# Seven products in place of eight for some blocks of a two-layer encoder's projections

## The chip, the core and the metric

The kernel runs on one core of one Trainium2 chip, and the metric is its device time in microseconds. A core has engines that work side by side, each through its own list of instructions in order: TensorE (PE) multiplies a stationary block of 128 x 128 with a moving one of up to 512 columns and adds into a bank of PSUM; VectorE (DVE) and ScalarE (ACT) work element by element; GpSimd (POOL) fills, masks and issues transfers here; SyncE (SP) issues transfers. Transfers are carried by 16 DMA engines. Engines wait for one another by semaphores. In shapes, 128x512 means 128 partitions with 512 elements each.

## What is computed

A trunk of one layer A and one layer B on x of 256 x 2048, all in float32, with 32 heads of 128 and an inner width of 4096:

```
h = rms_norm(x, a_norm);  q, k, v, g = split(h @ a_w_in, 4)          # 2048 -> 4 x 4096
o = chunked_relbias_attention(q, k, v, rel_bias)                     # chunks of 64, band of 9 chunks
x = x + (o * silu(g)) @ a_w_out                                      # 4096 -> 2048
h_kv = rms_norm(x, kv_norm);  k, v = split(h_kv @ kv_w, 2)
logf = log_sigmoid(h_kv @ f_w + f_b);  cum = cumsum(logf)
q, g = split(rms_norm(x, b_norm) @ b_w_in, 2)
o = forgetting_attention(q, k, v, cum)                               # causal, blocks of 128 queries
x = x + (o * silu(g)) @ b_w_out
return rms_norm(x, final_norm)
```

## The kernel before

**Matmuls.** Every float32 operand of a projection is split into a high part (rounded, type fp32r) and a low part (the rest), and a product is three matmuls: high by high, high by low, low by high. `mm3` (line 174) does this for one slice of 128 of the contraction and both halves t of the 256 rows; line 182 is the matmul, with the activations stationary and 512 columns of weights moving.

**Units and sub-blocks.** A *unit* (`Unit`, line 300) is one output of 256 x 512 in two PSUM banks. Its weights come in *sub-blocks* b of two slices (KB = 2), 512 KB each, so a sub-block is 2 slices x 2 halves x 3 = 12 matmuls. Layer A has 16 *pairs* of units g: `aqk` (q and k of two heads) and `avg` (v and gate of the same heads), eight sub-blocks each; layer B has 16 pairs `bqg` and `bkv`. The output projections of A (`ao`) and B (`bo`) are four units of sixteen sub-blocks. A matmul whose tile is called `aqk_acc` belongs to an aqk unit.

**Weights.** `Feed` (line 186) runs a fixed list of all sub-blocks. `begin` lets SP load one into one of RAW = 3 load buffers (line 203). `prepare` splits it into one of SPLIT = 4 pairs of split buffers: ACT copies the high part (line 237), DVE subtracts the low part (line 238); in layer B a gain is multiplied in (lines 232 and 233). `get` keeps four prepared ahead, so a split is written three sub-blocks before its matmuls and waits until PE has left the buffer.

**Attention beside the projections.** `attention` (line 394) is a generator; each `yield` ends a step, and tables (lines 55 to 61) say after which sub-block of a later unit how many steps are written. For a pair of layer A: qk is copied out of the banks by ACT with the row scale (`evac_scaled`, line 367); `turn` (line 355) transposes blocks of 32 on DVE (line 360) and sends 16 transfers (line 363), here 12 by POOL and 4 by ACT; q and k are split (lines 382, 383); PE does the scores s1p and s0p (lines 390 to 392, 414); DVE adds the bias and takes the maximum (421, 422); ACT does exp (424); the sums are inverted and the gate scaled (430 to 435); probabilities and gate are turned with 16 transfers of POOL (tiles sgY, sgZ); the probabilities are split; PE does the product with v (op, lines 390 to 392 and 448); DVE and ACT write the result (452 to 457). `close_vg` (line 559) splits v and forms the gate when the avg unit is complete. Scores stand behind the last avg sub-block (`QK_STEPS`), the second turn is written behind sub-block 1 of the next aqk unit (`PV_STEPS`), the split and op behind sub-blocks 0 and 2 of the next avg unit (`OLD_A_STEPS`). `feed.behind` (line 252) ties a split of attention to the weights' split before it.

**Order.** The source gives the order in which instructions are written. The builder (the Tile framework) then orders each engine's list, places tiles in their slots and sets the semaphores.

**Projections.** `project` (line 332) runs a list of sub-blocks with other generators beside it. `ao_closed` (line 623) adds x, stores x1 and turns it into the operand of layer B; the last unit is transposed on PE at once (`x_to_T`, lines 160 and 167). For the last bo unit the second half of its last eight sub-blocks is held back, so that the first half's rows are finished under it.

Of the kernel before, what the change touches and what calls it, by code (L numbers as in the profile page):

```python
# [16 lines left out]
P = 128  # L17
S = 256
# [23 lines left out]
RAW = 3  # L42
# [8 lines left out]
TERMS = 8  # L51
HEAT = 9
WAIT = 8

QK_STEPS = {0: 1, 6: 1, 7: 2}
PV_STEPS = {1: 1}
# [17 lines left out]
def trunk(ctx, tc, x, x_t, gains, a_w_in, a_rel, a_w_out, kv_w, f_w, f_b, b_w_in, b_w_out, final_norm, out):  # L74
# [99 lines left out]
    def mm3(acc, lhs, k, ts, hi, lo, nk, begun):  # L174
# [5 lines left out]
        for t, i in steps:  # L180
            x, w = parts[i]
            pe.matmul(acc[t], x[:, t * P:(t + 1) * P], w,  # L182
                      start=t not in begun, stop=k == nk - 1 and i == 2)
            begun.add(t)

    class Feed:
# [8 lines left out]
        def load(self, spec, b, first):  # L195
            if self.early:
                raw = self.early.pop(0)
            else:
                raw = stream.tile([P, IL, KB, HN], F32, name=f"{spec['name']}_raw{b}", tag="raw", bufs=RAW)
# [6 lines left out]
        def begin(self, first=None):  # L206
            spec, b = next(self.todo, (None, 0))
            if spec:
# [5 lines left out]
        def prepare(self, ahead=True, parts=(slice(None),)):  # L214
# [30 lines left out]
        def refill(self):  # L245
            while len(self.loaded) < RAW:
# [20 lines left out]
    def spec(name, w, nk, late=0, kept=0, g0=None):  # L267


        return dict(name=name, w=w, nk=nk, late=late, kept=kept, g0=g0)  # L270

    def whole(spec):
        return [(spec, b) for b in range(spec["nk"] // KB)]

    qkvg = []
    for g in range(NG):
        qkvg.append(spec(f"aqk{g}", a_w_in[2 * g], KD))
        qkvg.append(spec(f"avg{g}", a_w_in[2 * g + 1], KD))
# [3 lines left out]
    for sp_ in qkvg[2:]:  # L282
        todo += whole(sp_)
    ao = [spec(f"ao{u}", a_w_out[u], KI) for u in range(4)]
    for sp_ in ao:
        todo += whole(sp_)
# [6 lines left out]
    ao_order = [i for sp_ in ao for i in whole(sp_)]  # L293
    bo_order = [i for sp_ in bo for i in whole(sp_)]
    bo_order.insert(KI // KB + WAIT, bo_order.pop(KI // KB - 1))
    todo += bo_order
# [3 lines left out]
    class Unit:  # L300
# [3 lines left out]
        def __init__(self, lhs, sp_):  # L304
            self.lhs, self.nk, self.late = lhs, sp_["nk"], sp_["late"]
            self.acc = [ps_acc.tile([P, UN], F32, name=f"{sp_['name']}_acc{t}", tag="acc") for t in range(NT)]
            self.held, self.left, self.begun = [], self.nk // KB, set()

        def step(self, b):
            hi, lo = feed.get()  # L310
            hold = b >= self.nk // KB - self.late
            if hold:
                self.held.append((b, hi, lo))
            for j in range(KB):
                mm3(self.acc, self.lhs, b * KB + j, range(1 if hold else NT), cols(hi, j), cols(lo, j), self.nk,
                    self.begun)
# [532 lines left out]
```

## Time and profile before

| | us |
|---|---|
| median of three runs | 1760.83 |
| the three runs | 1760.07, 1760.83, 1763.58 |
| the profiled execution, device time | 1762.27 |
| its span in the trace | 1760.4 |

The granted clock of PE in the profiled execution is 0.998 of full speed. The program moves 396.34 MB, a mean of 225 GB/s. The page gives busy time of each engine, a chain of work followed back from the last instruction, and groups of instructions; the trace can be asked for who waited for whom, for instructions in order of time, and for the busy time of each engine in a stretch. A row such as `L369 ACT ACTIVATE qk<-bkv_acc,rstd_b 128x256 f32<-128x256 f32 x32 | 15.0, 473 | 11.4 <-PE` is: 32 instructions of line 369 on ACT, 15.0 us busy, 473 ns each, and 11.4 us in which the engine had stood idle just before them, ended by PE. PE's busy time counts overlapping matmuls, so the spacing of their starts is the better measure.

### The profile page before, as it was taken

How to read it: one execution, taken by the hardware profiler on the slowest of the kernel's cores; microseconds unless marked ns; L12 is line 12 of the kernel's file. 1: busy time of each engine (PE TensorE's matmuls, PEld its weight loads, DVE VectorE, ACT ScalarE, POOL GpSimd, SP SyncE). 2: the span in 40 equal slices, each digit the busy share in tenths (PEclk: the TensorE clock that was granted, in tenths of full speed). 3: DMA queues.
4: the chain of work that ended last, by engine and by line, in shares of the span. 5: the costliest groups of instructions: out<-in, count | busy, mean ns of one | idle time of the engine just before them, and what ended most of it. 6: DMA issues, size and time to landing. Idle time of an engine off the chain costs nothing.

```text
span 1760.4 us, 25526 instructions
## 1 busy us (share of the span) xinstructions
PE 1746.0 (99%) x8387; PEld 1533.1 (87%) x8387; DVE 1159.1 (66%) x1662; ACT 1084.1 (62%) x2063; POOL 515.7 (29%) x1071
## 2 busy tenths in 40 slices
PE   9999999999999999999999999999999999999997
PEld 7888888888888888888888888888888888888886
DVE  6666666666666666655666777777777777776654
ACT  6555555555555555555556777777777777765443
POOL 1333333333333333111104333333333333333000
PEclk9999999999999999999999999999999999999999
DMA  7867776777777777777766777777777777776665
GB/s 255 248 218 227 225 225 224 225 224 224 223 224 224 224 225 222 222 239 240 239 195 226 236 227 222 227 224 226 223 228 226 227 222 231 249 225 222 216 217 161
DMA packets 143652, 396.34 MB, mean 225 GB/s; under 512 B 31104, under 2 KB 38560, under 8 KB 143392
## 3 DMA queue, kind: packets, MB, share of 16 engines
q1 hardware_dynamic: 107472, 354.25, 63.8%
q0 software_dynamic: 32256, 37.29, 6.6%
q10 hardware_dynamic: 3792, 3.17, 0.6%
q8 instruction: 66, 1.08, 0.2%
q14 instruction: 66, 0.54, 0.1%
HBM read 351.05 MB, written 4.23 MB: 202 GB/s over the span
## 4 chain that ended last, share of the span: by engine, by line
PE 94%; DMA 2%; DVE 2%; ACT 1%; issue 0%; POOL 0%; SPq 0%; ACTq 0%; DVEq 0%; POOLq 0%
PE bkv_acc L182 19%; PE bqg_acc L182 19%; PE avg_acc L182 18%; PE aqk_acc L182 17%; PE ao_acc L182 9%; PE bo_acc L182 8%; DMA bo_raw<-in_b_w_out 1%; PE op L448 1%; PE s0p L414 1%; PE op L391 0%; PE s1p L390 0%; PE s1p L391 0%; PE op L392 0%; PE op L390 0%; PE s1p L392 0%
## 5 line engine op out<-in xcount | busy, mean ns | idle before, releaser
L363 POOL DMA_DIRECT2D sgZ<-sgY x512 | 250.9, 497 | 194.6 <-DVE sgY L360 96.5
L363 POOL DMA_DIRECT2D turned<-turned x448 | 219.9, 498 | 267.7 <-PE avg_acc L182 93.0
L233 DVE SCALAR_TENSOR_TENSOR bqg_lo<-bqg_raw,gain,bqg_hi 128x512 fp32r<-128x512 f32 x256 | 182.0, 747 | 97.1 <-ACT bqg_hi L232 97.0
L232 ACT ACTIVATE bqg_hi<-bqg_raw,gain 128x512 fp32r<-128x512 f32 x256 | 170.9, 714 | 114.1 <-PE bqg_acc L182 50.2
L238 DVE TENSOR_TENSOR avg_lo<-avg_raw,avg_hi 128x1024 fp32r<-128x1024 f32 x127 | 153.4, 1219 | 115.6 <-ACT avg_hi L237 115.5
L238 DVE TENSOR_TENSOR aqk_lo<-aqk_raw,aqk_hi 128x1024 fp32r<-128x1024 f32 x125 | 152.4, 1219 | 92.7 <-ACT aqk_hi L237 92.6
L233 DVE SCALAR_TENSOR_TENSOR bkv_lo<-bkv_raw,gain,bkv_hi 128x512 fp32r<-128x512 f32 x256 | 181.3, 748 | 45.3 <-ACT bkv_hi L232 42.3
L237 ACT ACTIVATE avg_hi<-avg_raw 128x1024 fp32r<-128x1024 f32 x127 | 132.5, 1055 | 124.5 <-PE aqk_acc L182 60.1
L182 PE MATMUL bqg_acc<-bqg_hi,x1Th 128*128 128x512 f32 x512 | 191.6, 384 | 0.0
L182 PE MATMUL aqk_acc<-aqk_hi,xTh 128*128 128x512 f32 x512 | 190.9, 383 | 0.2
L182 PE MATMUL aqk_acc<-aqk_lo,xTh 128*128 128x512 f32 x512 | 189.0, 379 | 1.2 <-DVE aqk_lo L238 1.2
L182 PE MATMUL avg_acc<-avg_hi,xTh 128*128 128x512 f32 x512 | 190.2, 382 | 0.0
L182 PE MATMUL avg_acc<-avg_lo,xTh 128*128 128x512 f32 x512 | 188.9, 379 | 0.3 <-DVE avg_lo L238 0.3
L182 PE MATMUL bqg_acc<-bqg_hi,x1Tl 128*128 128x512 f32 x512 | 189.1, 379 | 0.0
L182 PE MATMUL bkv_acc<-bkv_hi,x1Th 128*128 128x512 f32 x512 | 189.0, 379 | 0.0
L182 PE MATMUL aqk_acc<-aqk_hi,xTl 128*128 128x512 f32 x512 | 188.9, 379 | 0.0
L182 PE MATMUL avg_acc<-avg_hi,xTl 128*128 128x512 f32 x512 | 188.8, 379 | 0.0
L182 PE MATMUL bkv_acc<-bkv_lo,x1Th 128*128 128x512 f32 x512 | 188.8, 379 | 0.0
L182 PE MATMUL bkv_acc<-bkv_hi,x1Tl 128*128 128x512 f32 x512 | 188.8, 379 | 0.0
L182 PE MATMUL bqg_acc<-bqg_lo,x1Th 128*128 128x512 f32 x512 | 188.8, 379 | 0.0
L237 ACT ACTIVATE aqk_hi<-aqk_raw 128x1024 fp32r<-128x1024 f32 x125 | 131.5, 1052 | 91.9 <-PE avg_acc L182 44.0
L232 ACT ACTIVATE bkv_hi<-bkv_raw,gain 128x512 fp32r<-128x512 f32 x256 | 168.8, 711 | 27.9 <-PE bqg_acc L182 21.4
(205 smaller groups left out, 3442.4 us busy)
## 6 DMA issues: line engine op xcount, KB each, us to landing
bqg_raw<-in_b_w_in SPq DMA_DIRECT2D x128, 512.0 KB, 4.3
bkv_raw<-in_kv_w SPq DMA_DIRECT2D x128, 512.0 KB, 4.0
avg_raw<-in_a_w_in SPq DMA_DIRECT2D x127, 512.0 KB, 4.3
aqk_raw<-in_a_w_in SPq DMA_DIRECT2D x125, 512.0 KB, 3.4
ao_raw<-in_a_w_out SPq DMA_DIRECT2D x64, 512.0 KB, 4.2
bo_raw<-in_b_w_out SPq DMA_DIRECT2D x64, 512.0 KB, 4.2
sgZ<-sgY POOLq DMA_DIRECT2D x512, 40.0 KB, 4.0
turned<-turned POOLq DMA_DIRECT2D x448, 32.0 KB, 3.5
```

The costliest lines, as they stand in the source:

```text
L182: pe.matmul(acc[t], x[:, t * P:(t + 1) * P], w, start=t not in begun, stop=k == nk - 1 and i == 2)
L232: act.activation(hi[:, :, j], raw[:, :, j], AF.Copy, scale=gk)
L233: dve.scalar_tensor_tensor(lo[:, :, j], raw[:, :, j], gk, r32(hi[:, :, j]), op0=OP.mult, op1=OP.subtract)
L237: act.activation(hi[:, :, j], raw[:, :, j], AF.Copy)
L238: dve.tensor_sub(lo[:, :, j], raw[:, :, j], r32(hi[:, :, j]))
L363: queues[j].dma_start(out=r32(z)[j * SQ:(j + 1) * SQ, i], in_=y[i * SQ:(i + 1) * SQ, j])
L414: pe.matmul(s0p[:, i], q0[:, i], qkT[:, HG + i, 0], start=True, stop=True)
L448: pe.matmul(op[:, i, P:], v1[:, i * DH:(i + 1) * DH], pT[:, i, NT], start=False, stop=i == HG - 1)
```

## The change

A *quad* is a sub-block of two units together: two slices, two halves and two units make a 2 x 2 by 2 x 2 product of blocks. It is done after Winograd's form of Strassen's scheme with seven block products (`Quad.step`) in place of eight. Three of them are added into the units' own banks and four into other banks, p1, p5, p7 and p6; after the last quad of a run ACT and DVE add those up into four blocks, `comb`, which are added to the units' results when these close. The sums of activations are made once by DVE and ACT (`sum_up`), the sums of weights for each quad by DVE (`Quad.split`), which passes four entries through the split buffers: two, two, one and two blocks of 512 columns.

Quads stand in: each pair of layer A but the first, for sub-block 7 of both units, after three sub-blocks of the first (15); ao units 0 and 1 woven together, for sub-blocks 0 to 2, and ao units 2 and 3, for 0 to 4 (8); bo units 2 and 3, for 0 to 4 (5). Between two quads of a projection are three ordinary sub-blocks. In layer A the row scale of qk now goes with a DVE instruction that adds `comb`, and v and gate are read from `comb` after DVE has added the banks.

There are six load buffers for three, shared by quads and ordinary sub-blocks. Room for tiles comes from the tiles `turned` and `sq0`, whose uses move into the buffers of quads, and the scratch for the descriptors of POOL's transfers is set to 4096 bytes. The scores of layer A come behind sub-block 0 of the next first unit, and the second turn behind its sub-block 3. The last transposes of ao come behind sub-block 1 of the first bqg unit.

```diff
-RAW = 3
+RAW = 6
+SCRATCH = 4096
...
+QUADS = 5
...
-QK_STEPS = {0: 1, 6: 1, 7: 2}
-PV_STEPS = {1: 1}
+QUAD_STEP = 3
+SECOND_STEPS = {0: 1, 6: 1}
+FIRST_STEPS = {0: 2, 3: 1}
...
+            if isinstance(b, Quad):
+                b.raw = [self.load(u, b.b) for u in b.specs]
+                self.loaded += [(spec, (b, i), b.raw[i - 2] if i > 1 else None, (None, None)) for i in range(4)]
...
+            if not spec:
+                self.ready.append(b[0].split(b[1]))
+                self.refill()
+                return
...
-            while len(self.loaded) < RAW:
+            while sum(raw is not None for _, _, raw, _ in self.loaded) < RAW:
...
+    class Quad:
+        def __init__(self, all_, specs, b, first, last):
+            self.all, self.specs, self.b, self.first, self.last = all_, specs, b, first, last
+        def split(self, i):
+            one, two = self.raw
+            t = self.all.t[:, 0]
+            if not i:
+                dve.tensor_sub(t[:, :, 0], two[:, :, 0], one[:, :, 0])
+                dve.tensor_sub(t[:, :, 1], two[:, :, 1], two[:, :, 0])
+            src = [one, t, two[:, :, 1:], one][i]
+            n = src.shape[2]
+            hi = stream.tile([P, IL, KB, HN], F32R, name=f"quad_hi{i}", tag="hi", bufs=SPLIT)
+            lo = stream.tile([P, IL, KB, HN], F32R, name=f"quad_lo{i}", tag="lo", bufs=SPLIT)
+            act.activation(hi[:, :, :n], src, AF.Copy)
+            dve.tensor_sub(lo[:, :, :n], src, r32(hi[:, :, :n]))
+            if not i:
+                dve.tensor_sub(one[:, :, 0], two[:, :, 1], t[:, :, 0])
+                dve.tensor_sub(one[:, :, 1], one[:, :, 1], one[:, :, 0])
+            return hi, lo
+        def step(self, lhs, first, second):
+            q, b = self.all, self.b
+            def x(k, t):
+                return [v(b * KB + k)[:, t * P:(t + 1) * P] for v in (lhs.h, lhs.l)]
+            def sx(i):
+                return q.sums[b][:, 0, i], q.sums[b][:, 1, i]
+            def add(u, t, a, w, j):
+                dot3(u.acc[t], a, [cols(v, j) for v in w], t not in u.begun, not u.left)
+                u.begun.add(t)
+            def prod(p, a, w, j):
+                dot3(p, a, [cols(v, j) for v in w], self.first, self.last)
+            if self.first:
+                q.p = [bank(n) for n in ("p1", "p5", "p7", "p6")]
+            p1, p5, p7, p6 = q.p
+            first.left -= 1
+            second.left -= 1
+            w = feed.get()
+            prod(p1, x(0, 0), w, 0)
+            add(first, 0, x(1, 0), w, 1)
+            w = feed.get()
+            prod(p5, sx(0), w, 0)
+            prod(p7, sx(2), w, 1)
+            w = feed.get()
+            add(second, 0, sx(3), w, 0)
+            w = feed.get()
+            add(first, 1, x(1, 1), w, 1)
+            prod(p6, sx(1), w, 0)
+            if self.last:
+                c = q.comb
+                act.activation(c[:, 0], p1, AF.Copy)
+                dve.tensor_add(c[:, 3], c[:, 0], p6)
+                dve.tensor_add(c[:, 2], c[:, 3], p5)
+                dve.tensor_add(c[:, 1], c[:, 3], p7)
+                dve.tensor_add(c[:, 3], c[:, 1], p5)
...
+        def order(self, first, second, n, lead):
+            a, b = ([(sp_, i) for i in range(n, sp_["nk"] // KB)] for sp_ in (first, second))
+            normal = a[:-1] + b[:3] + a[-1:] + b[3:]
+            out = normal[:lead]
+            for i in range(n):
+                out.append((None, Quad(self, (first, second), i, not i, i == n - 1)))
+                out += normal[lead + 3 * i:lead + 3 * i + 3] if i < n - 1 else normal[lead + 3 * i:]
+            return out
+        def open(self, lhs, n):
+            self.t = big_tile([P, 2, IL, KB, HN], F32, f"{self.name}_quad")
+            self.comb = self.t.rearrange("p r a j n -> p (r a j n)").rearrange("p (i n) -> p i n", n=UN)
+            free = self.t[:, 1].rearrange("p a j n -> p (a j n)").rearrange("p (c s) -> p c s", c=2)
+            for b in range(n):
+                if b % 2 == 0:
+                    two = big_tile([P, 2, 2, 4, P], F32R, f"{self.name}_sums{b}")
+                self.sum_up(lhs, b, two[:, b % 2], free)
+                yield
+        def sum_up(self, lhs, b, dst, free):
+            self.sums[b] = dst
+            hi, lo = dst[:, 0], dst[:, 1]
+            xs, v = free[:, 0].rearrange("p (k s) -> p k s", s=S), free[:, 1].rearrange("p (i s) -> p i s", s=P)
+            k = b * KB
+            dve.tensor_add(xs, r32(lhs.hi[k // BIG][:, k % BIG:k % BIG + KB]),
+                           r32(lhs.lo[k // BIG][:, k % BIG:k % BIG + KB]))
+            a11, a21, a12, a22 = (xs[:, j, t * P:(t + 1) * P] for j in range(KB) for t in range(NT))
+            dve.tensor_add(v[:, 0], a21, a22)
+            dve.tensor_sub(v[:, 2], a11, a21)
+            dve.tensor_sub(v[:, 1], v[:, 0], a11)
+            dve.tensor_sub(v[:, 3], a12, v[:, 1])
+            act.activation(hi, v, AF.Copy)
+            dve.tensor_sub(lo, v, r32(hi))
...
+        qkvg.append(spec(f"aqk{g}", a_w_in[2 * g], KD, quads=g > 0))
+        qkvg.append(spec(f"avg{g}", a_w_in[2 * g + 1], KD, quads=g > 0))
...
+    a_quads = Quads("a", None)
+    a_pairs = [Quad(a_quads, qkvg[2 * g:2 * g + 2], KD // KB - 1, True, True) for g in range(1, NG)]
+    for quad in a_pairs:
+        first, second = (whole(sp_) for sp_ in quad.specs)
+        todo += first[:QUAD_STEP] + [(None, quad)] + first[QUAD_STEP:] + second
+    ao_quads, bo_quads = Quads("ao", a_w_out), Quads("bo", b_w_out)
+    ao_order = ao_quads.order(ao[0], ao[1], 3, 13) + ao_quads.order(ao[2], ao[3], QUADS, 4)
+    todo += ao_order
...
+    bo_order = whole(bo[0]) + whole(bo[1])
     bo_order.insert(KI // KB + WAIT, bo_order.pop(KI // KB - 1))
+    bo_order += bo_quads.order(bo[2], bo[3], QUADS, 4)
...
-    turned = big_tile([P, 2, NQ, 2 * HG * NT, SQ], F32, name="turned")
-    home = [turned[:, i] for i in range(2)]
+    a_quads.t, a_quads.comb = first[1], big_tile([P, 2 * NT, UN], F32, name="comb")
+    sums = big_tile([P, 2, 2, 4, P], F32R, name="sums")
+    home = [v.rearrange("p (i c u) -> p i c u", i=NQ, u=SQ) for v in
+            (first[1][:, 1].rearrange("p a j n -> p (a j n)"), sums[:, 1].rearrange("p a k s -> p (a k s)"))]
...
-        evac_scaled(accs["qk"], 0, UN, rsA, qk)
+        if g:
+            for t in range(NT):
+                dve.scalar_tensor_tensor(qk[:, t], accs["qk"][t], rsA[:, t:t + 1], a_quads.comb[:, t],
+                                         op0=OP.mult, op1=OP.add)
+        else:
+            evac_scaled(accs["qk"], 0, UN, rsA, qk)
...
+    def close_vg(accs, g):
+        if g:
+            for t in range(NT):
+                whole_ = a_quads.comb[:, NT + t]
+                dve.tensor_add(whole_, accs["vg"][t], whole_)
+                accs["vg"][t] = whole_
...
-            accs["qk"] = drive(unit(xT), prev, PV_STEPS)
-            vg = unit(xT)
+            first, second = (Unit(xT, next(order)) for _ in range(2))
+            def products():
+                a_pairs[g - 1].step(xT, first, second)
+                for t in range(NT):
+                    act.activation(a_quads.comb[:, t], a_quads.comb[:, t], AF.Copy, scale=rsA[:, t:t + 1])
+            accs["qk"] = drive(rest(first), prev, FIRST_STEPS, {QUAD_STEP - 1: products})
+            vg = rest(second)
...
-        accs["vg"] = drive(vg, prev, QK_STEPS, {}, old, OLD_A_STEPS)
-        close_vg(accs)
+        accs["vg"] = list(drive(vg, prev, SECOND_STEPS, {}, old, OLD_A_STEPS))
+        if not g:
+            a_quads.sum_up(xT, KD // KB - 1, sums[:, 0], a_quads.comb)
+        close_vg(accs, g)
...
+        dve.tensor_add(xin, xin, ao_quads.comb[:, u % 2 * NT:u % 2 * NT + NT])
...
-            finish(x_to_T([xin[:, t] for t in range(NT)], u * 4))
+            last.append(x_to_T([xin[:, t] for t in range(NT)], u * 4))
...
-    project(oA, ao_order, ao_begun, ao_closed, [(prev, [2, 6, 2, 1])])
+    project(oA, ao, ao_order, ao_begun, ao_closed, [(prev, [1, 0, 2, 6, 2, 1]), (ao_quads.open(oA, QUADS), [3, 1, 1, 2, 2])])
...
-        accs["qg"] = drive(unit(x1T), prev, B1_STEPS, {}, old, OLD_B_STEPS)
+        accs["qg"] = drive(unit(x1T), prev if g else last[0], B1_STEPS if g else {1: 99}, {}, old, OLD_B_STEPS)
...
+        if u > 1:
+            dve.tensor_add(xin, xin, bo_quads.comb[:, u % 2 * NT:u % 2 * NT + NT])
...
-    project(oB, bo_order, bo_begun, bo_closed, [(old, [1, 1, 0]), (prev, [4, 2, 1, 1, 1, 7, 2, 1])])
+    project(oB, bo, bo_order, bo_begun, bo_closed, [(old, [1, 1, 0]), (prev, [4, 2, 1, 1, 1, 7, 2, 1]),
+                                                 (bo_quads.open(oB, QUADS), [20, 2, 2, 2, 2])])
...
-    nc = bacc.Bacc("TRN2", target_bir_lowering=False, num_devices=1)
+    nc = bacc.Bacc("TRN2", target_bir_lowering=False, num_devices=1, dynamic_dma_scratch_size=SCRATCH)
```

More of the change, by code (lines that the diff above doesn't have):

```diff
@@ L182, in mm3 @@
             pe.matmul(acc[t], x[:, t * P:(t + 1) * P], w,
-                      start=t not in begun, stop=k == nk - 1 and i == 2)
+                      start=t not in begun, stop=last and i == 2)
             begun.add(t)
@@ L347, in project @@
                         steps.pop(0)
[L348 to L351 removed]
+            for u in us:
+                if not units[u].left:
+                    more = closed(u, units[u].acc)
+                    if more:
+                        sides.append(more)
         for side, _ in sides:
```

83 lines of the change are left out of this document (41 added, 42 removed).

## The prediction

> **What bounds the kernel now.** I began with the page's busy shares and its chain, then read PE's waits, then the chain in order of time.
>
> ```profile
> PE 1746.0 (99%) x8387; PEld 1533.1 (87%) x8387; DVE 1159.1 (66%) x1662; ACT 1084.1 (62%) x2063; POOL 515.7 (29%) x1071
> ...
> PE 94%; DMA 2%; DVE 2%; ACT 1%; issue 0%; POOL 0%; SPq 0%; ACTq 0%; DVEq 0%; POOLq 0%
> ...
> PE op L390 <- ACT wideh L382: 1.9, 1, 1.9
> PE heat L108 <- DVE zeros L105: 1.3, 1, 1.3
> PE aqk_acc L182 <- DVE aqk_lo L238: 1.2, 2, 0.9
> PE bo_acc L182 <- DVE bo_lo L238: 0.8, 1, 0.8
> PE avg_acc L182 <- DVE avg_lo L238: 0.3, 1, 0.3
> ...
> 142.80 20.72 PE aqk_acc L182 x96
> ...
> 738.91 139.86 PE ao_acc L182 x648
> ```
>
> PE is on 94% of the chain, and the five rows of waits (total, times, longest) are all that it waited for in the program: 5.5 us. Between them it is one closed stream: 648 matmuls in 139.86 us and 96 in 20.72 us are 215.8 ns each. So a matmul of 512 columns is worth 0.2158 us of the end, and work on other engines nothing until it holds that stream up. A sub-block (12 matmuls) is 2.59 us.
>
> **What goes.** A quad takes a sub-block of each of two units (24 matmuls) as seven products of three, so 21. There are 15 in layer A (one for each pair but the first), 3 + 5 in layer A's output projection and 5 in layer B's: 28 quads, 84 matmuls, 84 x 0.2158 = 18.13 us. The scores that come a sub-block later are the same matmuls.
>
> The Trainium skill, TensorE: Matmul & The Clock Gate, "Back-to-back issue gap", gives about 131 ns for a 512-column matmul in a sustained stream with weight loads; by that the 84 would be 11.0 us. The row of 648 disagrees, and the measurement decides.
>
> **What is added** falls on DVE and ACT, beside the stream. Durations, and the load of three stages (a layer A pair, A's output projection, B's):
>
> ```profile
> L237 ACT ACTIVATE aqk_hi<-aqk_raw 128x1024 fp32r<-128x1024 f32 x125 | 131.5, 1052 | 91.9 <-PE avg_acc L182 44.0
> ...
> L369 ACT ACTIVATE qk<-aqk_acc,rstd_a 128x512 f32<-128x512 f32 x32 | 21.3, 687 | 14.8 <-PE aqk_acc L182 12.9 <-POOL rstd_a L122 1.9
> ...
> L626 DVE TENSOR_TENSOR xin<-ao_acc,xin 128x512 f32<-128x512 f32 x8 | 5.1, 682 | 0.0
> ...
> L237 ACT ACTIVATE aqk_hi<-first 128x512 fp32r<-128x512 f32 x6 | 3.5, 620 | 2.3 <-DMA first<-in_a_w_in 2.3
> ...
> L507 DVE TENSOR_TENSOR sq<-sq 128x512 f32<-128x512 f32 x2 | 1.4, 688 | 0.0
> ...
> L238 DVE TENSOR_TENSOR aqk_lo<-aqk_raw,aqk_hi 128x1024 fp32r<-128x1024 f32 x8 | 9.8, 1219 | 6.2 <-ACT aqk_hi L237 6.2
> ...
> L421 DVE SCALAR_TENSOR_TENSOR sg<-s1p,tb 128x512 f32<-128x512 f32 x2 | 1.4, 692 | 0.7 <-PE s1p L392 0.7
> ...
> L422 DVE TENSOR_REDUCE nm<-sg 128x2 f32<-128x512 f32 (+1 forms) x2 | 1.0, 544 | 0.0
> L383 DVE TENSOR_TENSOR widel<-turned,wideh 128x256 fp32r<-128x256 f32 x2 | 0.8, 418 | 0.0
> ...
> L479 DVE SCALAR_TENSOR_TENSOR gs<-gs,avg_acc 128x256 f32<-128x256 f32 x2 | 0.7, 414 | 0.0
> ...
> L383 DVE TENSOR_TENSOR q1l<-turned,q1h 128x128 fp32r<-128x128 f32 x2 | 0.6, 284 | 0.0
> L467 DVE SCALAR_TENSOR_TENSOR vl<-avg_acc,rstd_a,vh 128x256 fp32r<-128x256 f32 x1 | 0.5, 475 | 0.0
> L421 DVE SCALAR_TENSOR_TENSOR sg<-s0p,tb 128x256 f32<-128x256 f32 x1 | 0.4, 415 | 0.0
> ...
> 361.42:405.20 43.78, 43.78 (x216) 38.63 (x214) 28.23 (x37) 25.86 (x48) 13.89 (x29) 1.00 0.72 225
> 711.85:878.80 166.95, 166.95 (x779) 146.16 (x778) 96.99 (x115) 85.08 (x132) 32.02 (x67) 1.00 0.74 237
> 1589.80:1751.90 162.10, 161.26 (x756) 140.82 (x754) 88.97 (x99) 75.23 (x101) 10.29 (x21) 1.00 0.65 207
> ```
>
> In the last three rows the columns behind the length are PE, weight loads, DVE, ACT, POOL, clock, DMA share. A quad's splits on DVE are four differences of 512 (4 x 0.69) and the low parts (3 x 1.22 + 0.69), 7.1 us in place of 2 x 1.22: +4.7. On ACT 3 x 1.05 + 0.62 in place of 2 x 1.05: +1.7.
>
> - Layer A's pair has on DVE besides: four sums out of the banks (4 x 0.68), qk, taken from ACT (2 x 0.69), sums for v and g (2 x 0.68). 28.2 + 4.7 + 2.7 + 1.4 + 1.4 = 38.4 us of 43.78 - 0.65 = 43.1 us, **89%**. ACT: 25.9 + 1.7 + 0.7 (copy of p1) + 1.2 (two scalings) - 1.3 = 28.2 us, 65%.
> - A's projection: eight quads 37.4, five operand sums (0.69 + 4 x 0.28 + 0.69 = 2.5) 12.5, bank sums twice 5.5, four additions of 1024 4.9. 97.0 + 60.3 = 157.3 us of 166.95 - 5.2 = 161.8 us, **97%**. Instructions back to back overlap by about 0.08 us (the 1.51 us transposition quoted below begins 1.44 us before its successor); so packed it is near 90%.
> - B's projection: 89.0 + 23.4 + 12.5 + 2.7 + 2.4 = 130 us of 158.9 us, 82%.
>
> DVE stays under PE in every stage, but where it was two thirds full it is nearly full. What is late next is a low part. A quad passes through the same four split buffers, which then hold 1.29, 1.29, 0.65 and 1.29 us of matmuls in place of 2.59 each:
>
> ```profile
> 369.52 1.06 ACT L237 ACTIVATE aqk_hi<-aqk_raw 128x1024 fp32r<-128x1024 f32 x1 [1.58 <-PE aqk_acc L182]
> ...
> 370.61 1.22 DVE L238 TENSOR_TENSOR aqk_lo<-aqk_raw,aqk_hi 128x1024 fp32r<-128x1024 f32 x1 [1.00 <-ACT aqk_hi L237]
> ...
> 12.00:24.00 12.00, 10.82 (x49) 9.01 (x49) 11.61 (x21) 11.95 (x23) 0.00 (x0) 1.00 0.88 342
> 361.42:375.00 13.58, 13.58 (x66) 11.92 (x65) 10.13 (x14) 8.82 (x20) 5.98 (x13) 1.00 0.77 232
> ...
> 18.83 0.48 PE L182 MATMUL aqk_acc<-aqk_lo,xTh 128*128 128x512 f32 x1 [0.85 <-DVE aqk_lo L238]
> ```
>
> A split begins when PE leaves its buffer (ACT waited for PE until 369.52, 0.33 us behind the end of the third sub-block from 361.42) and is done 0.33 + 1.06 + 0.03 + 1.22 = 2.64 us later. Today it is wanted three sub-blocks later, 7.77 us: 5.1 us to spare. The sub-block behind a quad takes the buffer of the quad's first part and is wanted after the other three: 1.29 + 0.65 + 1.29 + 0.22 (the second matmul reads its low part) = 3.45 us. **0.8 us to spare**, less than one low part of 1.22 us queued ahead of it.
>
> Bounds for what a quad stalls: nothing, as at 361.42 to 375, where DVE was 75% busy and PE full; and 1.2 us, as at 12 to 24, where DVE was 97% busy and PE 10.82 of 12. It can't gain here, since a quad only adds to splits. I counted the queue on DVE from a pair's start, packed: q and k splits 1.1, v and g 1.2 + 1.1, the quad's first part and its differences 2.3, scores 1.9, the other parts 2.9, and 1 us of waits for ACT. The last part ends at 11.5 us and is wanted at 12.4 (a sub-block, 1.17 of scores, two sub-blocks, three parts); the sub-block behind it ends at 13.0, wanted at 13.7. It just fits, and a gap of DVE breaks it. I take the 0.85 us of the row at 18.83 for one quad in four: 28 / 4 x 0.85 = 5.95 us.
>
> **What costs nothing.** Six load buffers: SP issues the same loads, three sub-blocks earlier, with the DMA engines 72% busy; at best the 0.8 us on bo_lo near the end goes. The first pair's operand sum (2.5 us) lies under its seven sub-blocks of v and g; if it were uncovered it would cost 2.5 once. The last transposes of A's projection move behind two sub-blocks of B, where there is no gap to win:
>
> ```profile
> 878.78 0.22 PE bqg_acc L182
> ...
> 879.10 0.41 PE xT L167 x2
> ```
>
> This also shows that the builder, not the source, sets the order on an engine: a matmul of B stands ahead of a transpose written before it.
>
> **The sum.** 1762.27 (the profiled execution: span 1760.4 and 1.87 around it) - 18.13 + 5.95 = 1750.1. The median shown is 1.44 us under that execution: **1748.7 us**. Without a stall it is 1742.7, less 0.8 1741.9.
>
> **Rivals.** B, *stalls give most back*: where the sub-block behind each quad finds one low part ahead of it, it is 1.22 - 0.8 = 0.4 us late: 28 x 0.4 = 11.2, so 1760.83 - 18.13 + 11.2 = 1753.9. The 97% speaks for it, the queue that just fits and the 82% against.
>
> C, *no change*: at 0.65 us a quad all is given back, 1760.8. DVE has then become the bound; the row at 12 to 24 shows that it can.
>
> D, *slower: the attention's product waits for its transposition*. The probabilities pass a DVE transposition, 16 transfers of POOL and a split before PE's op:
>
> ```profile
> 366.99 1.51 DVE L360 STREAM_TRANSPOSE sgY<-sg 128x1280 f32<-128x1280 f32 x1
> 368.43 1.18 DVE L238 TENSOR_TENSOR aqk_lo<-aqk_raw,aqk_hi 128x1024 fp32r<-128x1024 f32 x1
> ...
> 369.05 4.40 POOL L363 DMA_DIRECT2D sgZ<-sgY  x9 [6.39 <-DVE sgY L360]
> ...
> 376.85 0.98 POOL L363 DMA_DIRECT2D sgZ<-sgY  x2 [0.79 <-DMA sgZ<-sgY]
> ...
> 389.99 0.28 PE L390 MATMUL op<-wideh,vh 128*128 128x256 f32 x1
> ...
> sgZ<-sgY POOLq DMA_DIRECT2D x512, 40.0 KB, 4.0
> ```
>
> The last transfer is issued at 377.3 and lands 4.0 us later, and the split's first half takes 0.5: op could start at 381.9, 14.9 us after the transposition began. From the scores' end (361.42) to op it is 28.6 us now, and with the change six sub-blocks, a quad and three sub-blocks, 27.8. So the transposition must begin within 12.9 us of the scores' end; now it begins at 5.6. The change writes it behind the quad and a sub-block: in the queue above, the low parts ahead of it run to 15.4 us, the sums out of the banks to 17.9, one more low part to 19.1. The scores end at 2.59 + 1.17 = 3.8, so it begins 15.3 us behind them, 2.4 us late: 15 x 2.4 = 36, so 1778.7. It turns from gain to loss at 18.13 / 15 = 1.2 us a pair. Against it: the builder may take the transposition earlier, or set op behind another sub-block, as it did with the transposes above.
>
> E, *POOL's transfers are held back*: the scratch for their descriptors is set to 4096. Nine go out without a break today; if only two could be under way, 16 would take 8 x 4.0 = 32 us and a pair's 28 56 us against PE's 43.1, some 13 us more in each of 31 pairs of both layers: 2150 us. The one wait of POOL on its own transfers above, 0.79 us, is no sign of that.
>
> The Trainium skill, SBUF — State Buffer, "SBUF size: 192, 224, or 256?", sets 16 KiB aside for these rings, of which a quarter would stay. An estimate with the 16 B of a descriptor in its page DMA: Bandwidth & Descriptors, "Terms": 32 rows over 16 engines and a completion are 48 B of a ring for a transfer, so 4096 would hold 85. No run here shows the ring.
>
> **Chances.** Forecast 0.52 (1741.5 to 1751.5), B 0.18 (to 1757.3), C 0.10 (to 1764.4), D 0.15, E 0.05. A measurement of this kernel can tell about 0.2%, 3.5 us, from no change. So faster 0.70, same 0.10, slower 0.20; the forecast, B and C hold 0.80, which makes the range 1741.5 to 1764.4.
>
> **What would show it.** 84 fewer matmuls at an unchanged 215.8 ns; DVE near 38 us of a 43 us pair; PE's waits on low parts some 6 us more in all, behind quads. It is wrong if PE waits on wideh (D), on DVE in nearly every pair (B, C), or POOL on its own transfers (E), and wrong the other way if PE's waits stay near 5 us: then it is 1742.

## The result, and the profile after

The changed kernel takes 1844.2 us (median of five, 1841.18 to 1849.62) against 1760.83: a ratio of 1.0473, 95% interval 1.0460 to 1.0486. The prediction was 1748.7. Its span is 1841.6 us, its granted clock 0.979 (0.998 before). All ratios below compare undisturbed executions; one of e6 (5025 us, the profiled one, so that e6 has no pair) and one of e15 (3080 us) were disturbed and are left out.

From the page of the changed kernel, the busy times and the shares of the chain:

```profile
PE 1766.8 (96%) x8303; PEld 1541.4 (84%) x8303; DVE 1378.3 (75%) x2034; ACT 1132.9 (62%) x2148; POOL 516.7 (28%) x1071
...
PE 73%; DMA 9%; DVE 8%; issue 4%; POOL 4%; ACT 2%; SPq 0%; ACTq 0%; POOLq 0%; DVEq 0%
```

The 84 matmuls are gone (8387 less 8303). But PE holds 73% of the chain in place of 94%, and DMA, DVE and POOL, which had 2%, 2% and 0%, hold 21%: a path through the other engines now sets the end. What PE waited for (us, times, longest):

```profile
PE op L527 <- ACT wideh L519: 51.5, 15, 5.4
PE ao_acc L185 <- DVE ao_lo L249: 4.4, 3, 2.1
PE xT L170 <- DVE xin L785: 2.7, 2, 2.5
PE bo_acc L528 <- DVE quad_lo L295: 1.8, 1, 1.8
```

The 15 waits for wideh, one for each pair with a quad, are the prediction's rival D. The chain in order of time places the loss by stage; first the kernel before, then the changed one:

```profile
51.41 5.18 PE aqk_acc L182 x24
...
697.73 12.95 PE avg_acc L182 x60
...
880.60 20.07 PE bqg_acc L182 x93
```

```profile
50.88 2.59 PE aqk_acc L185 x12
...
787.23 2.59 PE ao_acc L185 x12
...
968.06 15.54 PE bqg_acc L185 x72
```

| stage | before | after | matmuls saved | lost |
|---|---|---|---|---|
| 15 pairs of layer A | 659.3 | 736.4 | 9.7 | **86.8** |
| A's projection (ends set back by the 3 and 24 matmuls of B already done) | 169.3 | 175.7 | 5.2 | **11.6** |
| layer B and the rest | 880.5 | 878.7 | 3.2 | 1.5 |

Layer A's pairs lose nearly everything. One of them, in order of time (start, length, engine, then idle time ahead and its releaser in brackets):

```profile
298.77 0.61 PE L551 MATMUL s0p<-sums,q 128*128 128x128 f32 x4
...
302.63 1.22 DVE L295 TENSOR_TENSOR quad_lo<-first,quad_hi 128x1024 fp32r<-128x1024 f32 x1
...
306.07 1.23 DVE L295 TENSOR_TENSOR quad_lo<-aqk_raw,quad_hi 128x1024 fp32r<-128x1024 f32 x1 [0.57 <-ACT quad_hi L294]
...
309.03 2.36 DVE L249 TENSOR_TENSOR aqk_lo<-aqk_raw,aqk_hi 128x1024 fp32r<-128x1024 f32 x2 [0.30 <-ACT aqk_hi L248]
311.31 0.68 DVE L338 TENSOR_TENSOR comb<-comb,p 128x512 f32<-128x512 f32 x1
...
314.24 1.51 DVE L497 STREAM_TRANSPOSE sgY<-sg 128x1280 f32<-128x1280 f32 x1
...
316.29 5.38 POOL L500 DMA_DIRECT2D sgZ<-sgY  x11 [13.27 <-DVE sgY L497]
323.49 1.96 POOL L500 DMA_DIRECT2D sgZ<-sgY  x4 [1.83 <-issue]
326.37 0.50 POOL L500 DMA_DIRECT2D sgZ<-sgY  x1 [0.92 <-DMA sgZ<-sgY]
...
330.14 0.72 ACT L519 ACTIVATE wideh<-sgZ 128x256 fp32r<-128x256 f32 x2 [4.19 <-DMA sgZ<-sgY]
...
330.61 0.58 PE L527 MATMUL op<-wideh,vh 128*128 128x256 f32 x1 [3.39 <-ACT wideh L519]
...
333.58 0.63 PE L185 MATMUL avg_acc<-avg_lo,xTh 128*128 128x512 f32 x1
```

The scores end at 299.38. The transposition begins 14.86 us later, behind low parts and three sums out of the banks; op comes 16.37 us after that, at 31.2 us. PE has 27.8 us of work for the meantime and stands for 3.39. The last row is a matmul behind op: the windows there (length, PE, weight loads, DVE, ACT, POOL, clock, DMA share, GB/s) show why it takes 0.63 us:

```profile
332.00:334.00 2.00, 2.00 (x9) 1.83 (x8) 2.00 (x2) 0.76 (x1) 1.52 (x4) 0.50 0.23 66
334.00:336.00 2.00, 2.00 (x6) 1.63 (x5) 0.87 (x3) 0.63 (x1) 0.00 (x0) 0.50 0.95 297
336.00:338.00 2.00, 2.00 (x8) 1.65 (x8) 1.21 (x2) 0.19 (x1) 0.00 (x0) 0.77 0.74 233
```

Behind the wait the granted clock is 0.50 for some 6 us. So a pair shows 3.4 us of wait and some 2.5 us at half clock over what its matmuls need.

### The profile page after: what moved, and what is told of

It reads as the page before. It is cut to its first block, busy times and chain, and to the rows that moved or that the text cites. A ratio compares the mean times of both kernels' runs of the same rounds, so it can differ in the third digit from the quotient of the medians.

```text
span 1841.6 us, 25819 instructions
## 1 busy us (share of the span) xinstructions
PE 1766.8 (96%) x8303; PEld 1541.4 (84%) x8303; DVE 1378.3 (75%) x2034; ACT 1132.9 (62%) x2148; POOL 516.7 (28%) x1071
## 4 chain that ended last, share of the span: by engine, by line
PE 73%; DMA 9%; DVE 8%; issue 4%; POOL 4%; ACT 2%; SPq 0%; ACTq 0%; POOLq 0%; DVEq 0%
PE bkv_acc L185 18%; PE bqg_acc L185 18%; PE avg_acc L185 11%; PE aqk_acc L185 8%; PE bo_acc L185 6%; DMA sgZ<-sgY 5%; PE ao_acc L185 3%; POOL sgZ L500 3%; DVE aqk_lo L249 2%; DMA sums<-first 1%; PE op L585 1%; DVE sgY L497 1%; DVE quad_lo L295 1%; ACT aqk_hi L248 1%; PE p L529 1%
## 5 line engine op out<-in xcount | busy, mean ns | idle before, releaser
L500 POOL DMA_DIRECT2D sums<-first x448 | 219.9, 498 | 166.9 <-PE bqg_acc L185 86.7
L248 ACT ACTIVATE avg_hi<-avg_raw 128x1024 fp32r<-128x1024 f32 x112 | 115.9, 1048 | 98.5 <-PE avg_acc L185 61.0
L185 PE MATMUL avg_acc<-avg_lo,xTh 128*128 128x512 f32 x452 | 173.1, 395 | 0.0
L185 PE MATMUL avg_acc<-avg_hi,xTl 128*128 128x512 f32 x452 | 171.4, 391 | 0.0
L185 PE MATMUL aqk_acc<-aqk_hi,xTh 128*128 128x512 f32 x452 | 167.5, 382 | 1.1 <-ACT aqk_hi L248 1.1
L249 DVE TENSOR_TENSOR avg_lo<-avg_raw,avg_hi 128x1024 fp32r<-128x1024 f32 x112 | 132.2, 1215 | 48.2 <-ACT avg_hi L248 48.2
L185 PE MATMUL aqk_acc<-aqk_lo,xTh 128*128 128x512 f32 x452 | 166.4, 380 | 1.0 <-DVE aqk_lo L249 1.0
L185 PE MATMUL aqk_acc<-aqk_hi,xTl 128*128 128x512 f32 x452 | 166.1, 379 | 0.0
L249 DVE TENSOR_TENSOR aqk_lo<-aqk_raw,aqk_hi 128x1024 fp32r<-128x1024 f32 x110 | 133.0, 1223 | 36.2 <-ACT aqk_hi L248 36.0
L248 ACT ACTIVATE aqk_hi<-aqk_raw 128x1024 fp32r<-128x1024 f32 x110 | 112.5, 1049 | 67.3 <-PE avg_acc L185 62.8
```

Source lines behind the costliest of these rows:

```text
L185: pe.matmul(acc[t], x[:, t * P:(t + 1) * P], w, start=t not in begun, stop=last and i == 2)
L248: act.activation(hi[:, :, j], raw[:, :, j], AF.Copy)
L249: dve.tensor_sub(lo[:, :, j], raw[:, :, j], r32(hi[:, :, j]))
L500: queues[j].dma_start(out=r32(z)[j * SQ:(j + 1) * SQ, i], in_=y[i * SQ:(i + 1) * SQ, j])
```

## The experiments

A pair's length, from one end of the scores to the next over 15 pairs, is the best single figure; the kernel before has 43.77 (over its last 14 pairs, since the first pair's scores stand two sub-blocks later than the others'), and 21 matmuls in place of 24 make 43.12. "Late" is from the scores' end to the transposition, in a typical pair. e15 and e18 compute other products than the kernel should: they show what a cost is, and are no versions to use.

| run | what | us | ratio to before (95%) | pair | late |
|---|---|---|---|---|---|
| | changed kernel | 1844.2 | 1.0473 (1.0460-1.0486) | 49.09 | 14.9 |
| e1 | transposition before the quad | 1796.2 | 1.0193 (1.0176-1.0210) | 46.05 | 9.3 |
| e2 | zeros ahead of op | 1841.7 | 1.0461 (1.0443-1.0479) | 48.72 | 15.9 |
| e3 | projections' quads only, op too early | 1773.7 | 1.0072 (1.0057-1.0087) | | |
| e4 | six buffers, scratch | 1760.4 | 0.9995 (0.9986-1.0005) | 43.77 | 5.3 |
| e5 | op two sub-blocks later | 1794.9 | 1.0189 (1.0174-1.0204) | 45.72 | 16.3 |
| e6 | e1, quad after five | 1780.8 | 1.0102 (1.0085-1.0119) | | |
| e7 | projections' quads only | 1764.5 | 1.0018 (1.0008-1.0028) | 43.77 | |
| e8 | e6, no quads in A's projection | 1772.0 | 1.0054 (1.0038-1.0070) | 44.78 | 7.7 |
| e9 | e8, scores later | 1814.7 | 1.0303 (1.0280-1.0327) | 47.36 | 9.1 |
| e10 | e9, quad after four | 1785.2 | 1.0135 (1.0117-1.0153) | 45.45 | 5.6 to 8.8 |
| e11 | e9, differences later | 1814.7 | 1.0303 (1.0287-1.0320) | 47.34 | |
| e12 | B's projection's quads only | 1757.6 | 0.9980 (0.9971-0.9988) | 43.77 | 5.3 |
| e13 | e8, differences later | 1779.4 | 1.0106 (1.0090-1.0121) | 45.09 | 7.7 |
| e14 | e13, quad after four | 1762.5 | 1.0008 (0.9999-1.0017) | 44.19 | 8.0 |
| e15 | e8, no differences (other products) | 1745.4 | 0.9910 (0.9895-0.9925) | 43.12 | 6.2 |
| e16 | e8, differences on POOL | 1769.5 | 1.0051 (1.0037-1.0066) | 44.50 | 7.9 |
| e17 | e16, quad after four | 1764.1 | 1.0015 (1.0006-1.0024) | 43.85 | 7.9 |
| e18 | e8, differences in one unit (other products) | 1757.9 | 0.9983 (0.9973-0.9993) | 43.92 | |

Without quads in layer A (e4, e7, e12) the pair is again that of the last 14.

### Is it the wait at op? (e1, e2, e5)

```
e1: -FIRST_STEPS = {0: 2, 3: 1}      +FIRST_STEPS = {0: 2, 2: 1}
e5: -OLD_A_STEPS = {0: 1, 2: 99}     +OLD_A_STEPS = {1: 1, 4: 99}
e2, in attention, for layer A:
         op = bank("op")
+        for i in range(16):
+            pe.matmul(op, zeros[:, :P], zeros[:, P:], start=i == 0, stop=i == 15)
```

> The step that scales the gate and turns sg is written one sub-block earlier, ahead of the quad's products. Theory (the product with v waits for the transposition, and the granted clock falls behind each wait): the transposition begins about 9 us behind the scores in place of 15.1, PE's waits for wideh go from 51.5 us to under 3, the granted clock from 0.979 back to 0.998, a pair from 49.1 us to 43.1 to 43.8, and the time from 1844 to 1748 to 1760. Rival (DVE is the bound, and any order of its work leaves PE waiting somewhere): the waits move to low parts, a pair stays over 47 us, the time over 1815.

> The changed kernel with the probabilities' split and the product with v two sub-blocks later (behind sub-block 4 of the second unit); the transposition stays where the change put it. There are then 33.0 us of PE's work from the scores to op, against the 31.1 us that op took in the changed kernel. Theory (op's wait is a loop of scores, transposition, transfers and op, and moving either end opens it; VectorE's queue around the quad is a second cost that the wait had covered): PE's waits for wideh under 5 us, a pair 43.8 to 45.5 us, waits on low parts behind the quads 10 to 30 us in all, 1763 to 1790 us. Rival (the wait at op was the only loss in layer A): a pair 43.1 to 43.5 us, under 1762.

Moving either end removes the waits for wideh altogether and 48 and 49 us, so the wait at op is shown. But neither came to its expectation. What PE now waits for most are low parts behind the quad, for e1

```profile
PE aqk_acc L185 <- DVE aqk_lo L249: 14.5, 16, 1.0
PE aqk_acc L528 <- DVE quad_lo L295: 8.8, 12, 0.8
```

and for e5

```profile
PE aqk_acc L528 <- DVE quad_lo L295: 11.2, 14, 1.1
...
PE s0p L551 <- ACT quad_hi L294: 3.5, 13, 0.3
```

so VectorE's queue around the quad is a second cost, 2.9 and 2.6 us a pair, that the wait had hidden: while PE stood, VectorE caught up. Not all of it lies at the quad's low parts: the scores' matmuls, from the first to the last, take 2.15 us a pair in e1 and 2.51 in e5, against 1.32 in the changed kernel, where PE waits among them for the splits of q and k, which stand in the same queue.

> Sixteen more matmuls of zeros into op's bank stand ahead of each product with v in layer A: 16 x 0.216 = 3.45 us of PE work where PE waited 3.43 us; nothing else is changed. Theory (of the 6.0 us that a pair is longer, 3.4 are the wait and 2.6 the granted clock that falls to 0.5 behind it): op starts as late as before, the clock stays at 0.998, a pair takes 46.5 us, the time is 1800 to 1810. Rival (matmuls behind op are slow for another reason, such as operands that come late): the clock or the spacing behind op stays as it is, 1840 to 1850. If the matmuls of zeros delay op itself, it is over 1850.

The zeros did their work: the clock is 0.995 and the waits for wideh 5.4 us in all. The time fell by no more than the intervals allow, so both theories fell: the rival had the time, but the clock did come back. The rows of one pair (PE's and VectorE's timeline, then the window behind op):

```profile
345.89 0.61 PE L552 MATMUL s0p<-sums,q 128*128 128x128 f32 x4
...
362.31 1.50 DVE L498 STREAM_TRANSPOSE sgY<-sg 128x1280 f32<-128x1280 f32 x1
...
375.10 3.40 PE L584 MATMUL op<-zeros 128*128 128x512 bf16 x15
378.15 0.47 PE L528 MATMUL op<-wideh,vh 128*128 128x256 f32 x1
```

```profile
380.10:384.00 3.90, 3.90 (x20) 3.42 (x19) 1.63 (x3) 0.14 (x1) 0.62 (x2) 1.00 0.65 204
```

PE is at full clock behind op (1.00), and from op to the next scores it takes 16.3 us, a mean of 15 pairs, in place of 17.8. But from the scores to op it now takes 32.4 in place of 31.3, because the transposition begins 15.9 us behind the scores and not 14.9. **The pair is a loop**: scores, VectorE's queue, transposition, transfers, op, the rest of the pair, scores. From op to the next transposition it is 32.3 us in place of 32.7, and VectorE is busy 26.4 us of that in both; from the transposition to op it is 16.5 in place of 16.4. A faster PE only meets VectorE's queue sooner. The half clock is a symptom; it costs little of its own.

### Buffers and projections alone (e3, e4, e7, e12)

```
e4, from the kernel before: -RAW = 3   +RAW = 6 ; dynamic_dma_scratch_size=4096
e7: no quads in layer A's pairs, its steps as before; both projections keep theirs
e3: as e7, with [1, 0, 2, 6, 2, 1] in project in place of [2, 6, 2, 1]
e12: as e7, with  ao_order = [i for sp_ in ao for i in whole(sp_)]
```

> The kernel before with six load buffers and the scratch of 4096 alone, no quads. Theory (buffers and scratch cost nothing): 1757 to 1763 us. Rival (the scratch holds back the transfers of POOL, so that sgZ lands later): the time between a transposition and its op grows beyond 14.9 us, or POOL waits on its own transfers for more than 1 us a pair; over 1766, and up to 2150 if only two can be under way.

Rival E is out: six buffers and the small scratch cost nothing.

> The quads of layer A's pairs and their later scores are taken out; the 13 quads of the two output projections, six load buffers and the scratch stay. Theory (what is lost is lost at op, and the output projections give back about 5 us in waits of the 13 x 3 x 0.2158 = 8.4 us that they save): 1752 to 1760 us, PE's waits for wideh under 4 us. Rival (the weave of two units in the output projections, or six buffers, costs by itself): over 1766.

> As e3_projections (no quads in layer A's pairs), but with the last pair's attention at the sub-blocks of the output projection where the kernel before has it; in e3_projections its product with v came six sub-blocks too early and waited 7.2 us. Theory (the quads of A's output projection cost about 11 us in waits for the 5.2 us that they save, those of B's give back their 3.2 us in full): 1760 to 1766 us. Rival (weaving the units costs nothing once the product is back): 1750 to 1756 us.

e3 had the last pair's steps at the wrong sub-blocks, and its op waited 7.2 us; e7 mends that and is 9 us faster. It is still a little slower than before.

> Quads in B's output projection alone, five of them; layer A's pairs and A's output projection as in the kernel before, with six load buffers and the smaller scratch. Theory (the matmul sum is right where VectorE has room, 82% by the prediction's count): 5 x 3 x 0.2158 = 3.2 us saved and up to 1 us from the transposes that move, 1756 to 1759 us, a little less than before. Rival (each group of quads costs what it saves): 1760 to 1763 us.

**e12 is faster than the kernel before**, by 0.2%: 3.1 us where the 15 matmuls of B's projection are worth 3.2, so there the sum holds. Between e7 and e12 lie the eight quads of A's projection: they save 5.2 us and the time is some 7 longer with them, so they lose about 12, as the stage table had it. VectorE, counted at 97% there (by the trace it is busy 141 us of 174.5), was no place for them.

### What the second cost is (e6, e8 to e11)

```
e6: e1 and   -QUAD_STEP = 3   +QUAD_STEP = 5
e8: e6, ao_order as in e12
e9: e8, FIRST_STEPS = {1: 2, 3: 1}
e10: e9, QUAD_STEP = 4
e11: e9, the four dve.tensor_sub of Quad.split under "if i == 1" in place of "if not i"
```

> The transposition early as in e1_turn_early, and the quad behind five sub-blocks of the first unit in place of three, so that softmax and transposition lie ahead of its splits and not among them. Theory (in e1_turn_early PE waits about 2 us a pair, because VectorE has no gap from the pair's start to the sub-block behind the quad): these waits fall from about 32 us to under 10, a pair takes 43.1 to 44 us, the time is 1752 to 1775. Rival (VectorE is too full wherever the quad stands): waits on low parts stay over 25 us and the time over 1785.

> As e6_quad_later, and A's output projection without quads, its four units one behind another. Theory: 5 to 8 us less than e6_quad_later, since the waits on ao_lo and quad_lo in that stage (about 8 us with the clock behind them) and the wait for the last x go, against 5.2 us of matmuls that come back. Rival (they cost nothing): 5 us more than e6_quad_later.

e6 came out between its theory and its rival: 15 us less than e1 for the quad's place. e8 is 9 us under e6, a little more than its theory had. A pair of e8 still takes 44.78, 1.66 us too long. The scores' matmuls take 2.35 us of it in place of 1.32, so that 1.0 of the 1.66 us is lost among them, where PE waits most for the low part of k:

```profile
PE s1p L528 <- DVE widel L520: 4.5, 4, 1.9
```

> As e8_later_no_ao, with scores and softmax one sub-block later still (behind the second of the first unit) and the gate's scaling and transposition behind the fourth, just ahead of the quad. Theory (what is left in e8_later_no_ao, 44.8 us a pair in place of 43.1, is scores that wait for the splits of q and k, and a start-up gap behind each wait): these waits go, a pair takes 43.2 to 43.8 us, op still waits for nothing (7 us to spare there, 2.6 used), 1750 to 1758 us, a little less than before. Rival (the transposition again stands in the quad's low parts, as in e1_turn_early): waits on quad_lo of 1 us a pair, over 1768.

> As e9_scores_later with the quad behind the fourth sub-block in place of the fifth, so that the sums out of the banks have a sub-block more until qk is needed. Theory (the quad needs distance from softmax): waits on quad_lo grow, 2 to 15 us more than e9_scores_later. Rival (the quad needs distance from the evacuation of qk, whose lateness makes q and k late): a few us less.

> As e9_scores_later, with the quad's four differences written with its second part in place of its first. In e8_later_no_ao VectorE stands 2.6 us a pair at the first difference, waiting for the load of the second unit's weights, with low parts queued behind it. Theory (this wait holds up low parts): the wait on the load falls below 1 us a pair and the time by 3 to 10 us against e9_scores_later. Rival (VectorE has the time there): within 3 us of it.

e9 was wrong by some 60 us. I had counted 7 us to spare at op, and e8's trace has 4.2: the first half of the split ends 16.4 us behind the start of the transposition and op begins 20.6 behind it. Scores a sub-block later took 2.6 of them, the transposition came 1.4 us later behind the scores, and its transfers had landed 17.8 us after it began in place of 15.8, so op waited again:

```profile
PE op L527 <- ACT wideh L519: 14.5, 15, 2.2
```

e10 gave 30 us back, against its theory. e11 changed nothing there, with op again the limit.

### The differences (e13 to e18)

In e8 VectorE stands idle at the quad's first difference, for a load that SP issued 4.7 us before (timeline of SP and VectorE):

```profile
357.88 0.33 SPq L207 DMA_DIRECT2D avg_raw<-in_a_w_in  x1
...
362.59 0.69 DVE L288 TENSOR_TENSOR first<-avg_raw,aqk_raw 128x512 f32<-128x512 f32 x1 [2.58 <-DMA avg_raw<-in_a_w_in]
```

With six buffers the loads do not run ahead: the next waits until VectorE has left a buffer, and the quad needs two at once. The longest of SP's waits from 50 to 700 us:

```profile
SPq L207 <- DVE avg_lo L249: 197.5, 97, 5.0
SPq L207 <- DVE aqk_lo L249: 130.4, 86, 3.8
SPq L207 <- DVE quad_lo L295: 122.1, 30, 6.6
```

```
e13: e8, differences under "if i == 1" ; e14: e13, QUAD_STEP = 4
e15: e8 without the four differences, src = [one, two, two[:, :, 1:], one][i]
e16: e8 with pool.tensor_sub ; e17: e16, QUAD_STEP = 4
e18: e8 with "one" for "two" in the differences
```

> As e8_later_no_ao, with the quad's four differences written with its second part in place of its first, so that VectorE no longer stands at the load of the second unit's weights (2.6 us a pair) in front of the splits of q and k. Theory (a held queue): scores no longer wait for widel, a pair goes from 44.8 to 43.5 to 44.2 us, 1753 to 1763 us. Rival (amount of work): within 3 us of e8_later_no_ao, 1769 to 1775 us.

> As e13_diffs_later2 with the quad behind the fourth sub-block in place of the fifth. Theory (the place of the quad against softmax decides): waits on quad_lo of 0.5 to 1 us a pair, 6 to 15 us more than e13_diffs_later2. Rival (the lateness of qk at the unit's end decides): 2 to 8 us less.

> As e8_later_no_ao with the quads' four differences of weights left out (the raw weights are split in their place, so the quads compute other products): 2.8 us less of VectorE's work a pair and in each quad of B's projection, the same matmuls. If the amount of work is the bound, a pair falls to 43.1 to 43.4 us and the time to 1745 to 1752 us; if the place and the load behind the differences are, it is within 3 us of e13_diffs_later2.

> As e8_later_no_ao, with the quad's four differences taken within the first unit's weights (other products are computed): the same four instructions on VectorE, that no longer wait for the load of the second unit's weights. If that wait is what costs, a pair takes 43.1 to 43.4 us as in e15_no_diffs and the time is 1745 to 1750 us; if the work is, it stays within 4 us of e8_later_no_ao, 1768 to 1776 us.

e13 was 7 us slower, not faster: the first difference stayed where it was on VectorE (4.9 us ahead of the scores' end in both), only the last came later. e14 was 17 us faster than e13, where its theory had it slower: with the quad one sub-block earlier the order on VectorE is another. Its first difference stands 6.0 us ahead of the scores' end and its load is waited for 19.8 us in all (4.9 and 38.3 in e13); its first parts follow the softmax directly. The place is worth more than I could reason out.

e15 is the decisive one. All that PE waited for in it:

```profile
PE aqk_acc L185 <- DVE aqk_lo L249: 1.3, 2, 1.0
PE heat L111 <- DVE zeros L108: 1.3, 1, 1.3
PE aqk_acc L185 <- ACT aqk_hi L248: 1.1, 3, 0.6
```

and its first and last scores, 15 pairs apart, are 43.12 us a pair:

```profile
54.53 0.61 PE L545 MATMUL s0p<-sums,q 128*128 128x128 f32 x4
...
701.27 0.61 PE L545 MATMUL s0p<-sums,q 128*128 128x128 f32 x4
```

So the matmul sum holds in layer A to the hundredth, in the same order with the same quads, once VectorE is spared the four differences: 34.3 us busy a pair, against 36.6 in e8. e18 keeps this work; its wait for a load stayed (38.3 us against 39.3, in 650 us), but came 1.1 us earlier before the scores. It gained about half of e15's 26.6 us. Its time lies between what it should be if the load is the cost and what it should be if the work is, so e18 does not part them.

> As e8_later_no_ao with the four differences of each quad on POOL in place of VectorE. POOL's rows show 0.44 us for 256 elements, so about 0.9 us for 512, 3.5 us a pair beside the 13.9 us that it is busy. Theory (2.8 us of VectorE's work and its wait for the load of the second unit's weights, in front of the splits of q and k, are what a pair loses): a pair takes 43.1 to 43.5 us as in e15_no_diffs, 1745 to 1753 us, the first version with all of layer A's quads that is faster than the kernel before. Rival (POOL's differences come late or slow VectorE down, and the parts that need them wait): waits on quad_hi or quad_lo of 1 us a pair, over 1760 us.

> As e16_pool_diffs with the quad behind the fourth sub-block in place of the fifth (the place at which e14_quad4_early did best). If VectorE's relief is enough the place no longer matters: within 3 us of e16_pool_diffs. If softmax and quad still meet, 5 to 15 us more.

POOL is no way out. Its differences take 1.3 to 2.3 us and not 0.9, and VectorE is held beside them. e17 was 5 us faster than e16, where its two readings had it equal or slower, and still no faster than the kernel before. POOL's and VectorE's timeline in e16:

```profile
288.44 2.20 POOL L298 TENSOR_TENSOR aqk_raw<-aqk_raw 128x512 f32<-128x512 f32 x1
...
289.41 1.77 DVE L295 TENSOR_TENSOR quad_lo<-avg_raw,quad_hi 128x512 fp32r<-128x512 f32 x1
```

That low part takes 0.65 us, the mean of 15, in e17, where the two do not meet. Its end, 291.18, is 0.54 us behind POOL's, 290.64, and it ends 0.54 to 0.55 us behind POOL's in each of the 15 pairs of e16: it hardly advanced until POOL was through. VectorE's sums of 128x512 that read one operand from PSUM (comb<-avg_acc,comb) took 0.67 to 0.68 us beside POOL's differences and were not held. The Trainium skill, SBUF — State Buffer, "SBUF: two separate sides", says that VectorE with two SBUF operands and GpSimd share a pair of ports under an exclusive lock; these rows agree.

## Why the prediction was wrong

**What went** was right: 84 matmuls at 215.8 ns. e12 (B's projection) and e15 (layer A's pairs) show that they are worth their full price where nothing else is late.

**The step that failed** is in rival D, and it is not its arithmetic: "in the queue above, the low parts ahead of it run to 15.4 us, the sums out of the banks to 17.9, one more low part to 19.1 ... so it begins 15.3 us behind them, 2.4 us late". It begins 14.9 us behind them. The step that failed is the next sentence: "Against it: the builder may take the transposition earlier, or set op behind another sub-block, as it did with the transposes above." It did neither. I set a guess against a count of my own: the sum holds nothing for op's wait, which measured 51.5 us and brought the half clock with it, and D got a chance of 0.15.

**D's size** was short. 36 us were priced; the waits are 51.5, because the way from the transposition to op took 16.4 us and not 14.9: in the pair shown POOL's 16 transfers had pauses of 1.83 and 0.92 us. And D was priced as if PE went on at full speed behind its wait. It did not (some 2.5 us a pair at half clock), and e2 shows why restoring the clock does not give that back: D is a loop, and what PE gains behind op it loses again in front of it.

**Low parts** were taken at 5.95 us, one quad in four 0.85 us late. The count "it just fits" was for a pair that nothing else holds up. With op out of the way the quads lose 2.6 to 2.9 us a pair (e5, e1), more than B's 0.4 and C's 0.65. The queue that I counted has 2.3 us for the quad's first part and its differences, which is room for two of the four; in the pair shown the other two stand ahead of the pair's start. The load behind the first difference was not in it at all, and is 2.6 us of VectorE's time a pair in e8.

**89% of a pair** was read as room. It is 38.4 us of work by the count, 36.6 by e8's trace, in 43.1 with an order in it: e8 has the same work as e9 and e14 and differs by 42.7 us from the one and 9.5 from the other.

**A's projection** was warned of (97%) and then given 8/28 of 5.95 us; it lost 11.6. **B's projection**, at 82%, did as summed (e12). **Six buffers and scratch** cost nothing, as said (e4). **The transposes that move** were put at nothing too; in the changed kernel PE waits 2.5 us for xin there (the row of xT above), and in e12, without quads in A's projection, it does not.

What stays open: how the differences' work and their load share the last 1.7 us of a pair in e8; and whether there is an order with layer A's quads that beats the kernel before. e14 comes nearest and is the same within its interval. The one version found that is faster and computes the right products is e12, with no quads in layer A.

## What to carry to other kernels

When a change moves a step, add up the whole loop that the step is in, from its trigger round to the next trigger, and compare it with the bound engine's work; where your own count says late, don't set hope in the scheduler against it. Work put on an engine that is two thirds full is free only if it has no waiting readers just then: ask which instructions queue behind it, and which load it waits for itself. Try the cheapest stage first and alone: here one stage of three carried its gain.

## What the hardware showed besides

- The granted clock fell at PE's 15 waits of 2.4 to 5.4 us for wideh (to 0.50 in the pair shown; each of the 15 pairs took 17.3 to 18.7 us from op to the next scores), behind one of 2.15 us on ao_lo (0.83 over the 10 us around it) and, in e8, behind one of 1.57 us (0.72 from 456 to 462 us). In the changed kernel it stayed at 1.00 behind waits of 0.9 and 1.3 us, and also behind one of 2.46 us for xin (966 to 971 us), so the length of a wait alone does not tell here whether the clock falls. The Trainium skill, TensorE: Matmul & The Clock Gate, "What's actually happening", puts the fall behind an idle window of about 3.4 us; here less was enough.
- A VectorE subtraction of 128x512 from two SBUF operands took 0.65 us alone and 1.77 us beside a POOL subtraction of the same size, which itself took 1.3 to 2.3 us.
- Matmuls of zeros in a wait keep the clock up (0.995 in e2) and are no gain when the wait is part of a loop.
